# Block sums of four weight tiles made ahead in the memory-key stage, and two more seven-product pairs in the first feed-forward's first group

## The chip, the cores and the metric

The kernel runs on one core of a Trainium2 chip. A core has a matrix engine (TensorE, PE in the profile, whose weight loads are shown apart as PEld), a vector engine (VectorE, DVE), an activation engine (ScalarE, ACT), a general one (GpSimd, POOL) and a sync engine (SP), which here only issues transfers; 16 DMA engines carry those. The metric is the device time of one execution in microseconds. Before the change the median of three runs is 2403.33 us (2403.15 to 2403.53).

## The reference

The reference is one layer of a streaming encoder block on 256 tokens of width 2048, in float32:

```python
x = x + 0.5 * swiglu(rms_norm(x, ffn1_norm[l]), ffn1_w_up[l], ffn1_w_down[l])
h = rms_norm(x, mix_norm[l])
proj = h @ w_in[l]
...
x = x + cross_attention(rms_norm(x, xattn_norm[l]), rms_norm(mem, mem_norm[l]), ...)
x = x + 0.5 * swiglu(rms_norm(x, ffn2_norm[l]), ffn2_w_up[l], ffn2_w_down[l])

def swiglu(h, w_up, w_down):
    gate, up = jnp.split(h @ w_up, 2, axis=-1)
    return (jax.nn.silu(gate) * up) @ w_down
```

Two parts matter here. The memory's keys are `rms_norm(mem) @ wkv[:, :2048]` for 256 memory tokens, and the first feed-forward multiplies 256 tokens by `w_up` of 2048 x 11264.

## The kernel before, in words

**Numbers.** TensorE multiplies a rounded type (fp32r). Each float32 operand is split into a high part, which ACT makes by rounding (`split`, L153), and a low part, which VectorE makes as the rest (L154). A product is then three matmuls: high by high, high by low and low by high. Weights come as tiles of 128 x 2048 (1024 KB), which SP loads into a buffer named `raw`; the high part goes to `h`, the low to `l`. Each of the three has three buffers; within the first feed-forward there is a fourth, `raw1`.

**The stream of weights.** All tiles of the kernel stand in one list, `plan`, in the order in which they are used: tiles 0 to 15 for the memory's values, 16 to 31 for the memory's keys (wk0 to wk15 below), and from 32 on the first feed-forward. `weights` hands them out and keeps two prepared ahead; `prepare` issues a tile's load, its split, and what else its kind needs. `rest[i]` hangs side work on tile i: in the keys these are the loads and operands of x for the first feed-forward (xf, xg, xs, xd). The order in which each engine takes its instructions, and the buffer that each tile gets, are fixed when the program is built; at run time each engine takes its instructions in that order and waits by semaphores.

**The memory's keys.** Each tile is one `product`: 16 matmuls of 512 columns with the high part (L370) and 16 of 256 columns with the low part (L373). The result is summed (ACT L412, VectorE L414), split (L438, L439) and after every second tile stored by POOL's queue (L988).

**The first feed-forward.** The up projection runs in 11 groups of 512 gate and 512 up columns. A group has eight tiles, called pairs, since each holds two blocks of 128 rows of the weights by two blocks of 512 columns. `FIRST` gives for each group the order of its pairs and the kind of each. A mixed pair ("m") is multiplied in the plain way, 8 products or 24 matmuls, from one split of its tile; its operands include a difference of two blocks of x ("less", xd), which is made for the pairs in `BOTH`. A fast pair ("f") needs 7 products, 21 matmuls, in the manner of Strassen's scheme, but sums of its four weight blocks: VectorE makes them in three instructions (`td`: L337 with 1024 columns, L339 and L341 with 512), ACT and VectorE split the upper 1536 columns of the tile (`h`, `l`) and the 2048 columns of the sums in two halves (`th`, `tl`). `three` issues the matmuls, highs at L709 and lows at L711. All products of a group add into eight banks of the accumulator memory; when a group is done, ACT and VectorE take them out (`ev`, L791 to L804), and the next group's banks come free by that.

**Sums made ahead.** In the second feed-forward some fast pairs are of a third kind, "ready" (`sums_ready`): their sums were made earlier, in the middle of the kernel, and are kept in device memory in a tile t. `make_ahead` does it: POOL's queue loads the tile (L224), VectorE makes four subtractions of 512 columns in place (L229), POOL's queue stores the result (L230). There it works in a pool of its own, `prep`, of two buffers. `beside` calls its steps between the tiles, one pair per four tiles, each finished three tiles after its start. A ready pair loads two raw tiles, the upper 1536 columns of its weights (768 KB) and t (1024 KB), and VectorE only makes the low parts.

Of the kernel before, what the change touches and what calls it, by code (L numbers as in the profile page):

```python
# [8 lines left out]
F32 = mybir.dt.float32  # L9
# [4 lines left out]
P = 128  # L14
# [5 lines left out]
NG = DFF // 512  # L20
# [22 lines left out]


PIECES = "f1 a3 f0 a4 f2 a5 a6 f7"
FIRST = ["m0 f1 m2 f3 f5 m4 f7 m6"] + ["f1 f3 M0 f4 f2 M6 f5 f7"] * 2 + ["f1 f3 M0 a4 f2 a5 a6 f7"] + [PIECES] * (NG - 4)
KINDS = {"m": "mixed", "M": "mixed", "f": "fast", "a": "fast"}


# [7 lines left out]
def first(g):  # L57
    return [(KINDS[e[0]], g, int(e[1])) for e in FIRST[g].split()]

# [22 lines left out]
def adds(name, e):  # L82

    return e[0] == "fast" and (name == "ffn1" or e[1] > 3) and f"a{e[2]}" in FIRST[e[1]]


def sums_ready(name, e):

    made = {0: (), 1: (6,), 2: (5, 7), 3: (5, 7)}.get(e[1], range(8))
    return name == "ffn2" and e[0] == "fast" and e[2] not in made  # L90

# [2 lines left out]
def block_kernel(ctx: ExitStack, tc: tile.TileContext, xT, xin, memT, vec, gfin, bgate, lruw, wu1, wd1, win, wv,  # L94
# [15 lines left out]
    scoped = {}  # L110
# [49 lines left out]
    plan, ahead, made_ahead = [], [], []  # L160
    orders = {"ffn1": ffn_order(), "ffn2": ffn_order(every=True)}

    def plan_ffn(name, wu, wd):
        for e in orders[name]:
            src = wd[e[4], e[3]] if e[0] == "down" else wu[e[1], e[2]]
            kind = "fast" if e[0] == "fast" else "plain"
            if name == "ffn1" and e[0] == "mixed" and f"M{e[2]}" in FIRST[e[1]]:
                kind = "added"
            if e[0] == "down" and e[4] < NG - 1 and e[4] % 2 == 0 and e[3] % 2 and (e[4] or name == "ffn1"):
                kind = "added"  # L170
            if kind == "fast" and name == "ffn2" and e[1] < 4:
                kind = "fast early"
            if adds(name, e):
                kind += " added"
            if sums_ready(name, e):
                kind = "ready"
                t = kept.tile([P, 2048], F32, name=f"t{e[1]}_{e[2]}")
                made_ahead.append((src, t))
                src = src, t
            plan.append(((name,) + e, src, kind))  # L180
# [15 lines left out]
    first_ffn = len(plan)  # L196
# [23 lines left out]

    def make_ahead(src, to):

        t = scoped["prep"].tile([P, 2048], F32, name="prep", tag="prep")
        nc.gpsimd.dma_start(t, src)  # L224
        yield
        b = [t[:, i * 512:(i + 1) * 512] for i in range(4)]
        with tc.issue_after(done["low"]):
            for o, x, y in ((1, 0, 1), (0, 0, 2), (2, 2, 1), (3, 3, 2)):
                dve.tensor_tensor(out=b[o], in0=b[x], in1=b[y], op=ALU.subtract)  # L229
        nc.gpsimd.dma_start(to, t)  # L230
        yield

    under_way = []

    def beside(i):

        if under_way and (i >= under_way[0][0] or "prep" not in scoped):
            next(under_way.pop(0)[1])
        if made_ahead and "prep" in scoped and i >= turn[0] and i < first_second - 4 and (
                not first_q - 12 <= i < first_q + 5):  # L240
            turn[0] = i + 4
            steps = make_ahead(*made_ahead.pop(0))
            next(steps)
            under_way.append((i + 3, steps))
# [5 lines left out]
    def weights(*key, most=2):  # L250
        while plan and len(ahead) < most:
            i = next(planned)
            k, src, kind = plan.pop(0)
            if i == 0:
                in_turn.enter_context(tc.manual_schedule(engines={sp.engine, act.engine, dve.engine}))
            if i == 0:
                begun.append(raw_tile())
                act.dma_start(begun[0][:, :512], in_blocks(src, 512)[:P])
            if i < len(head):
                head[i]()  # L260
            if plan and plan[0][2] == "added":
                begun.append(begin_added(plan[0][1]))
            ahead.append((k, prepare(src, kind, i if i < 4 else None)))
            if i in rest:
                rest[i]()
            beside(i)
            if i == 7:
                in_turn.close()
        k, w = ahead.pop(0)
        assert k == key, (k, key)  # L270
        return w
# [7 lines left out]
    def raw_tile():  # L279

        if "raw2" in scoped and next(loads) % 5 > 2:
            return scoped["raw2"].tile([P, 2048], F32, name="raw2", tag="raw2")
        if "raw1" in scoped and next(loads) % 4 == 3:
            return scoped["raw1"].tile([P, 2048], F32, name="raw1", tag="raw1")
        return rawp.tile([P, 2048], F32, name="raw", tag="raw")
# [285 lines left out]
        for z in range(2):  # L571
            act.activation(g[:, z * T:][:, :T], a[:, z * T:(z + 1) * T], ACT.Copy, scale=gain(k + z))

    BOTH = [0, 2, 4, 6]

    def operand_pairs(src, gain, q, xg, out, every=False):


        for a in src:
# [6 lines left out]
            if every and q == 3:  # L586
                if not i:
                    xd.append(slot(F32R, "xd"))
                less = [xd[-1][:, a:a + 256] for a in (512 * i, 512 * i + 256)]
            if not every and 2 * q + i in BOTH:  # L590
                n = 512 * (BOTH.index(2 * q + i) % 2)
                if not n:
# [133 lines left out]
    def ffn(name, pairs, sq, then, begin=(), sums=()):  # L726
# [38 lines left out]
        for at, e in enumerate(order):  # L765
# [3 lines left out]
            if kind != "down":  # L769
# [3 lines left out]
                for i, (a, b, n) in enumerate(PRODUCTS["ready" if sums_ready(name, e) else kind]):  # L773
                    u = uses[g, n]
                    if u[0] == (p, i):
                        accs[n] = bank()
                    own, less = pairs[p]
                    products.append((accs[n], part(own, a, P) if a >= 0 else part(less, -1 - a, P), part(w[b // 4] if fast else w, b % 4, 512),
                                     u[0] == (p, i), u[-1] == (p, i)))
# [826 lines left out]
```

## Time and profile before

| | before |
|---|---|
| median of 3 runs | 2403.33 us |
| the profiled execution: its time / its span | 2403.28 / 2401.5 us |
| TensorE busy | 2391.5 us, 12044 matmuls |
| VectorE busy | 2081.6 us |
| ACT busy | 1568.6 us |
| memory's keys begin on TensorE at | about 94 us |
| first feed-forward begins on TensorE at | 182.66 us |
| second group of the first feed-forward at | 224.02 us |

Times in the rows are microseconds from the start of the span. A row of the timeline is: start, duration, engine, line, operation, output and inputs by the program's names, type and shape; in brackets at its end stand the idle time just before it and what ended it. Matmuls overlap, so a duration of 0.39 us does not mean that the next one starts 0.39 us later. A row of transfers gives what is loaded, the queue, the size, and the time from issue to landing.

### The profile page before, as it was taken

The numbers are of one execution on the slowest core, as the hardware profiler recorded it, in microseconds if no ns is written. First come the engines' busy times: TensorE is split into PE (matmuls) and PEld (weight loads), VectorE is DVE, ScalarE is ACT, GpSimd is POOL, SyncE is SP. The second block draws the span as 40 slices with busy tenths as digits, with TensorE's granted clock in tenths as the row PEclk, the third lists the DMA queues.
The fourth block names the chain that finished last, engine by engine and source line by source line (L and its number), as shares of the span: only waits on it lengthen the run. The fifth ranks groups of instructions, "written<-read, shape, count | busy, mean of one in ns | idle before, by whom it ended". The sixth has DMA issues, their size and how long they took to land.

```text
span 2401.5 us, 31008 instructions
## 1 busy us (share of the span) xinstructions
PE 2391.5 (100%) x12044; PEld 1990.1 (83%) x12044; DVE 2081.6 (87%) x2368; ACT 1568.6 (65%) x1609; POOL 120.2 (5%) x174
## 2 busy tenths in 40 slices
PE   9999999999999999999999999999999999999998
PEld 8888888888888888888888888888888888888887
DVE  7769999999999878778778888876799999999995
ACT  7756777777777665445457556655676677777774
POOL 0000000000000000000000000010000000000000
PEclk9999999999999999999999999999999999999999
DMA  8876888898999755676776868885687899999993
GB/s 310 310 248 224 270 268 266 273 277 273 276 277 276 264 190 208 250 270 254 276 307 250 315 241 268 301 297 216 212 332 292 317 277 276 273 278 273 265 278 133
DMA packets 98740, 640.04 MB, mean 267 GB/s; under 512 B 10976, under 2 KB 11488, under 8 KB 32928
## 3 DMA queue, kind: packets, MB, share of 16 engines
q1 hardware_dynamic: 74160, 493.61, 54.8%
q0 software_dynamic: 24288, 144.19, 24.6%
q8 instruction: 94, 1.54, 0.2%
q14 instruction: 54, 0.44, 0.0%
q10 hardware_dynamic: 144, 0.26, 0.0%
HBM read 601.18 MB, written 36.83 MB: 266 GB/s over the span
## 4 chain that ended last, share of the span: by engine, by line
PE 97%; DVE 2%; DMA 1%; issue 0%; ACT 0%; ACTq 0%; DVEq 0%
PE acc L709 39%; PE acc L711 20%; PE acc L370 11%; PE acc L396 6%; PE acc L397 6%; PE acc L402 6%; PE acc L373 6%; PE acc L749 1%; PE acc L554 1%; DVE l L154 0%; DVE tl L154 0%; DMA raw<-wq 0%; PE acc L1368 0%; PE acc L1112 0%; PE acc L1393 0%
## 5 line engine op out<-in xcount | busy, mean ns | idle before, releaser
L153 ACT ACTIVATE h<-raw 128x2048 fp32r<-128x2048 f32 (+3 forms) x423 | 684.8, 1633 | 400.0 <-PE acc L397 115.5
L154 DVE TENSOR_TENSOR l<-raw,h 128x2048 fp32r<-128x2048 f32 (+2 forms) x365 | 749.3, 2054 | 197.2 <-ACT h L153 193.9
L709 PE MATMUL acc<-h,xh 128*128 128x512 f32 x1221 | 474.2, 391 | 0.7 <-ACT h L153 0.6
L709 PE MATMUL acc<-h,xl 128*128 128x512 f32 x1221 | 473.8, 390 | 0.0
L153 ACT ACTIVATE h<-td 128x1024 fp32r<-128x1024 f32 x290 | 304.6, 1056 | 177.8 <-PE acc L709 65.2
L154 DVE TENSOR_TENSOR tl<-td,h 128x1024 fp32r<-128x1024 f32 x290 | 352.3, 1220 | 13.1 <-ACT h L153 11.3
L709 PE MATMUL acc<-h,hidop 128*128 128x512 f32 x1408 | 351.7, 391 | 0.0
L709 PEld LDWEIGHTS acc<-h,hidop 128*128 128x128 f32 x1408 | 262.7, 188 | 54.0
L709 PEld LDWEIGHTS acc<-h,xh 128*128 128x128 f32 x1221 | 229.2, 188 | 53.4 <-ACT h L153 4.7
L709 PEld LDWEIGHTS acc<-h,xl 128*128 128x128 f32 x1221 | 229.3, 188 | 46.5
L370 PE MATMUL acc<-ops,h 128*128 128x512 f32 x896 | 218.0, 393 | 0.0
L396 PE MATMUL acc<-h,ops 128*128 128x512 f32 x512 | 201.2, 393 | 0.0
L397 PE MATMUL acc<-h,ops 128*128 128x512 f32 x512 | 199.4, 390 | 0.0
L711 PE MATMUL acc<-tl,xh 128*128 128x512 f32 x660 | 193.6, 395 | 0.1
L370 PEld LDWEIGHTS acc<-ops,h 128*128 128x128 f32 x896 | 164.0, 188 | 32.4
L711 PE MATMUL acc<-l,hidop 128*128 128x512 f32 x704 | 190.6, 389 | 0.0
L337 DVE TENSOR_TENSOR td<-raw 128x1024 f32<-128x1024 f32 x149 | 181.6, 1218 | 3.5 <-DMA raw<-wout 2.3
L711 PE MATMUL acc<-l,xh 128*128 128x512 f32 x561 | 157.0, 390 | 0.0
L711 PEld LDWEIGHTS acc<-l,hidop 128*128 128x128 f32 x704 | 132.1, 188 | 27.6
L711 PEld LDWEIGHTS acc<-tl,xh 128*128 128x128 f32 x660 | 120.2, 188 | 34.4 <-DVE tl L154 11.0
L402 PE MATMUL acc<-l,ops 128*128 128x512 f32 x512 | 126.6, 389 | 0.0
L711 PEld LDWEIGHTS acc<-l,xh 128*128 128x128 f32 x561 | 105.3, 188 | 22.4
(276 smaller groups left out, 3094.8 us busy)
## 6 DMA issues: line engine op xcount, KB each, us to landing
raw<-wu SPq DMA_DIRECT2D x151, 1024.0 KB, 7.1
raw<-wd SPq DMA_DIRECT2D x88, 1024.0 KB, 7.4
l<-wu POOLq DMA_DIRECT2D x59, 768.0 KB, 8.5
raw<-win SPq DMA_DIRECT2D x40, 1024.0 KB, 4.8
raw<-wg SPq DMA_DIRECT2D x32, 1024.0 KB, 5.8
prep<-wu POOLq DMA_DIRECT2D x25, 1024.0 KB, 6.6
t<-prep POOLq DMA_DIRECT2D x25, 1024.0 KB, 4.7
raw<-t SPq DMA_DIRECT2D x25, 1024.0 KB, 6.2
```

The costliest lines, as they stand in the source:

```text
L153: done["high"] = act.activation(h, raw, ACT.Copy).ins
L154: done["low"] = dve.tensor_tensor(out=l, in0=raw, in1=h.bitcast(F32), op=ALU.subtract).ins
L337: dve.tensor_tensor(out=two[0], in0=raw[:, None, :512].broadcast_to([P, 2, 512]), in1=two[1], op=ALU.subtract)
L370: pe.matmul(acc, h[:, k * P:(k + 1) * P], xs[k], start=k == 0, stop=False)
L373: done["product"] = pe.matmul(acc[:, :T], l[:, k * P:(k + 1) * P], xs[k][:, :T], start=False, stop=k == KT - 1).ins
L396: pe.matmul(accs[t], x[:, t * P:][:, :P], h[j], start=first and j == 0, stop=False)
L397: pe.matmul(accs[t], x[:, T + t * P:][:, :P], h[j], start=False, stop=False)
L402: done["product"] = pe.matmul(accs[t], x[:, t * P:][:, :P], l[j], start=False, stop=last and j == 3).ins
L554: pe.transpose(acc[:, z * T + t * P:][:, :P], tile[:, t * 512 + (2 * y + z) * P:][:, :P], ident)
L709: pe.matmul(acc, a, b, start=start, stop=False)
L711: done["product"] = pe.matmul(acc, ah, bl, start=False, stop=stop).ins
L749: pe.transpose(acc[:, z * T + t * P:][:, :P], hid[t][:, (2 * y + z) * P:][:, :P], ident)
```

## The change

Four things are changed, and one follows from them.

1. In the first group of the first feed-forward the pairs 4 and 6, mixed before, become fast (`FIRST`).
2. The fast pairs 1, 3, 5 and 7 of that group become ready: their sums are made ahead. `beside` starts one of the four with each of the tiles wk1, wk5, wk9 and wk13, and finishes it two tiles later.
3. In this stage there is no `prep` pool, so `make_ahead` takes a tile from `raw_tile`, that is, one of the three raw buffers.
4. The operand "less" is no longer made for pair 4 (`BOTH`).

The line numbers from L240 on are nine higher in the changed kernel (L337 is L346, L709 is L718, L802 is L811); those of `split` are two higher (L153 is L155), `make_ahead` five (L229 is L234).

```diff
-FIRST = ["m0 f1 m2 f3 f5 m4 f7 m6"] + ["f1 f3 M0 f4 f2 M6 f5 f7"] * 2 + ...
+FIRST = ["m0 f1 m2 f3 f5 f4 f7 f6"] + ["f1 f3 M0 f4 f2 M6 f5 f7"] * 2 + ...
...
 def sums_ready(name, e):
 
+    if name == "ffn1":
+        return e[0] == "fast" and e[1] == 0 and e[2] in (1, 3, 5, 7)
     made = {0: (), 1: (6,), 2: (5, 7), 3: (5, 7)}.get(e[1], range(8))
     return name == "ffn2" and e[0] == "fast" and e[2] not in made
...
     def make_ahead(src, to):
 
-        t = scoped["prep"].tile([P, 2048], F32, name="prep", tag="prep")
+        if "prep" in scoped:
+            t = scoped["prep"].tile([P, 2048], F32, name="prep", tag="prep")
+        else:
+            t = raw_tile()
         nc.gpsimd.dma_start(t, src)
...
     def beside(i):
 
-        if under_way and (i >= under_way[0][0] or "prep" not in scoped):
+        if under_way and (i >= under_way[0][0] or "prep" not in scoped and i > first_ffn):
             next(under_way.pop(0)[1])
+        if i in range(first_ffn - 15, first_ffn, 4):
+            steps = make_ahead(*made_ahead.pop(0))
+            next(steps)
+            under_way.append((i + 2, steps))
...
-    BOTH = [0, 2, 4, 6]
+    BOTH = [0, 2, 6]
```

Three places of the engines' orders show how the instructions move. The first is POOL, which issues the transfers of its queue; before, in the stages of the memory's values (v, the last two of them) and keys (k):

```order
L971 DMA v6_137<-vs_964 128x1024
L971 DMA v7_138<-vs_970 128x1024
L988 DMA k0_123<-ops_960 128x1024
L988 DMA k1_124<-ops_1073 128x1024
L988 DMA k2_125<-ops_1179 128x1024
L988 DMA k3_126<-ops_1296 128x1024
L988 DMA k4_127<-ops_1390 128x1024
```

and now:

```order
L980 DMA v7_142<-vs_976 128x1024
L229 DMA raw_1152<-wu1 128x2048
L997 DMA k0_127<-ops_966 128x1024
L997 DMA k1_128<-ops_1084 128x1024
L229 DMA raw_1366<-wu1 128x2048
L997 DMA k2_129<-ops_1191 128x1024
L235 DMA t0_3_96<-raw_1152 128x2048
L997 DMA k3_130<-ops_1309 128x1024
L997 DMA k4_131<-ops_1405 128x1024
L229 DMA raw_1596<-wu1 128x2048
L235 DMA t0_5_97<-raw_1366 128x2048
```

Between the stores of the keys stand now the loads of the tiles made ahead (wu1 is the weight of the first feed-forward) and the stores of their sums (t0_3 is pair 3's of group 0).

The second is SP at the last key tiles, with the semaphores that each load waits for; DMAHW stands for completions of SP's own queue, DMASW for those of POOL's. Before, from wk11 to wk15 and m0:

```order
L310 DMA raw_1452<-wk 128x2048 [waits DMAHW2_49,DVE_49]
L310 DMA raw_1516<-wk 128x2048 [waits DMAHW3_49,DVE_49]
L876 DMA xf_1305<-xT 128x1024 [waits DMAHW1_49]
L310 DMA raw_1569<-wk 128x2048 [waits DMAHW4_49,DVE_49]
L310 DMA raw_1615<-wk 128x2048 [waits DMAHW5_49,DVE_49]
L310 DMA raw_1661<-wk 128x2048 [waits DMAHW6_49,DVE_49]
L310 DMA raw_1707<-wu1 128x2048 [waits DMAHW0_49,DVE_49]
```

and now, from wk11 to wk15, m0, f1 with its sums, and m2:

```order
L319 DMA raw_1468<-wk 128x2048 [waits DMASW3_49,DMASW0_49,DVE_49]
L319 DMA raw_1537<-wk 128x2048 [waits DMAHW4_49,DVE_49]
L319 DMA raw_1590<-wk 128x2048 [waits DMAHW6_49,DVE_49]
L319 DMA raw_1638<-wk 128x2048 [waits DMAHW0_49,DVE_49,Activation_49]
L319 DMA raw_1684<-wk 128x2048 [waits DMAHW2_49,DMASW6_49,DMASW4_49]
L319 DMA raw_1735<-wu1 128x2048 [waits DMAHW1_49,DVE_49]
L335 DMA raw_1794<-wu1 128x1536 [waits DMAHW2_49,DVE_49]
L337 DMA raw_1796<-t0_1_95 128x2048 [waits DMAHW5_49,DMAHW3_49,DVE_49]
L319 DMA raw_1836<-wu1 128x2048 [waits DMAHW4_49,DVE_49]
```

The loads of wk11 and of wk15 wait now for transfers of POOL's queue, and between m0 and m2 stand two loads in place of one.

The third is VectorE in the first group. Before, from f1's sums to f3's:

```order
L337 TENSOR_TENSOR td_1768<-raw_1766 128x1024
L339 TENSOR_TENSOR td_1768<-raw_1766,td_1768 128x512
L341 TENSOR_TENSOR td_1768<-raw_1766,td_1768 128x512
L154 TENSOR_TENSOR tl_1777<-td_1768,h_1776 128x1024
L337 TENSOR_TENSOR td_1842<-raw_1840 128x1024
L154 TENSOR_TENSOR l_1812<-raw_1810,h_1811 128x2048
L154 TENSOR_TENSOR tl_1777<-td_1768,h_1776 128x1024
L339 TENSOR_TENSOR td_1842<-raw_1840,td_1842 128x512
```

and now, from m2's low part to f4's sums:

```order
L156 TENSOR_TENSOR l_1838<-raw_1836,h_1837 128x2048
L156 TENSOR_TENSOR l_1871<-raw1_1866,h_1870 128x1536
L156 TENSOR_TENSOR tl_1875<-raw_1868,h_1874 128x1024 x2
L156 TENSOR_TENSOR l_1909<-raw_1904,h_1908 128x1536
L156 TENSOR_TENSOR tl_1913<-raw_1906,h_1912 128x1024 x2
L346 TENSOR_TENSOR td_1941<-raw1_1939 128x1024
L348 TENSOR_TENSOR td_1941<-raw1_1939,td_1941 128x512
L156 TENSOR_TENSOR l_1946<-raw1_1939,h_1945 128x1536
L350 TENSOR_TENSOR td_1941<-raw1_1939,td_1941 128x512
```

Sums (td) stood with every second pair before; now the first of them in the group are f4's, behind the low parts of m2, f3 and f5.

More of the change, by code (lines that the diff above doesn't have):

```diff
@@ L45 @@
 PIECES = "f1 a3 f0 a4 f2 a5 a6 f7"
-FIRST = ["m0 f1 m2 f3 f5 m4 f7 m6"] + ["f1 f3 M0 f4 f2 M6 f5 f7"] * 2 + ["f1 f3 M0 a4 f2 a5 a6 f7"] + [PIECES] * (NG - 4)
+FIRST = ["m0 f1 m2 f3 f5 f4 f7 f6"] + ["f1 f3 M0 f4 f2 M6 f5 f7"] * 2 + ["f1 f3 M0 a4 f2 a5 a6 f7"] + [PIECES] * (NG - 4)
 KINDS = {"m": "mixed", "M": "mixed", "f": "fast", "a": "fast"}
```

## The prediction

> **What bounds the kernel now.** I read the busy shares and the chain of waits on the page first, then the table of busy time by stretch for the two places that the change touches: the memory's keys (about 94 to 183 us) and the first feed-forward's first group (from 183 us).
>
> ```profile
> PE 2391.5 (100%) x12044; PEld 1990.1 (83%) x12044; DVE 2081.6 (87%) x2368; ACT 1568.6 (65%) x1609; POOL 120.2 (5%) x174
> PE 97%; DVE 2%; DMA 1%; issue 0%; ACT 0%; ACTq 0%; DVEq 0%
> ...
> 100.00:200.00 100.00, 100.00 (x554) 87.11 (x553) 72.47 (x99) 56.84 (x75) 5.33 (x10) 1.00 0.75 255
> 182.66:230.00 47.34, 47.34 (x209) 38.60 (x208) 44.57 (x45) 31.27 (x28) 1.42 (x2) 1.00 0.71 232
> ```
>
> TensorE is busy for 2391.5 of 2401.5 us, so a removed matmul is a gain and an added wait of TensorE is a loss, nearly one for one. The last two rows (columns: span, then busy time of PE, PEld, DVE, ACT and POOL, granted clock, DMA share, GB/s) say where slack is: in the keys VectorE works 72% of the time and the transfers take 75% of the engines' time; in the first group VectorE works 44.57 of 47.34 us. The change takes subtractions out of the second stretch, puts two "fast" pairs into it, and loads the first.
>
> **The gain: six matmuls.** A pair by eight products is 24 matmuls, by seven 21.
>
> ```profile
> 218.58 0.39 PE L709 MATMUL acc<-h,xh 128*128 128x512 f32 x1
> 224.02 0.39 PE L709 MATMUL acc<-h,xh 128*128 128x512 f32 x1
> ```
>
> These are the first matmuls of m6 and of the next group's first pair: 5.44 us for 24, so 0.2267 us each. Two pairs turned from m to f give 6 x 0.2267 = 1.36 us. That TensorE has nothing else to win is seen from the one wait in this stretch, quoted below: 0.60 us.
>
> **VectorE's bill in the first group.** The distance from one start to the next is what an instruction costs on this engine (the first five rows; the last three are ACT's, for the high parts):
>
> ```profile
> 204.73 2.28 DVE L154 TENSOR_TENSOR l<-raw,h 128x2048 fp32r<-128x2048 f32 x1
> 206.93 1.22 DVE L154 TENSOR_TENSOR tl<-td,h 128x1024 fp32r<-128x1024 f32 x1
> 208.06 0.69 DVE L339 TENSOR_TENSOR td<-raw,td 128x512 f32<-128x512 f32 x1
> 208.66 1.75 DVE L154 TENSOR_TENSOR l<-raw,h 128x1536 fp32r<-128x1536 f32 x1
> 210.33 0.69 DVE L341 TENSOR_TENSOR td<-raw,td 128x512 f32<-128x512 f32 x1
> 136.46 1.91 ACT L153 ACTIVATE h<-raw 128x2048 fp32r<-128x2048 f32 x1 [0.57 <-PE acc L370]
> 231.14 1.06 ACT L153 ACTIVATE h<-td 128x1024 fp32r<-128x1024 f32 x1 [0.18 <-DVE td L341]
> 232.85 1.50 ACT L153 ACTIVATE h<-raw 128x1536 fp32r<-128x1536 f32 x1 [0.17 <-ACT hidop L753]
> ```
>
> So 2048 columns cost 2.20 us, 1536 cost 1.67, 1024 cost 1.13 and 512 cost 0.60. A mixed pair is 2.20. A fast pair is 1.13 + 0.60 + 0.60 for its sums, 1.67 and 2 x 1.13 for its low parts: 6.26. A ready pair needs no sums: 1.67 + 2.26 = 3.93. Before, the group (m0 f1 m2 f3 f5 m4 f7 m6) is 4 x 2.20 + 4 x 6.26 = 33.8; now (m0, four ready, m2, f4, f6) 2 x 2.20 + 4 x 3.93 + 2 x 6.26 = 32.6. Over the whole group VectorE is hardly relieved: what the four ready pairs save (4 x 2.33 = 9.3) f4 and f6 take back (2 x 4.06 = 8.1). And the work is later: the ready pairs stand at the front, the pairs with sums to make at the end. ACT gets 1.50 + 2 x 1.06 in place of 1.91 for each new fast pair, 3.4 us in a stretch where it works 31.27 of 47.34; that and the operand that BOTH no longer makes, in the keys, are within slack and count nothing.
>
> **The keys: sixteen subtractions and 8.4 MB.** Each of the four tiles made ahead costs four subtractions, a 1 MB load and a 1 MB store on POOL's queue.
>
> ```profile
> L229 DVE TENSOR_TENSOR prep<-prep 128x512 f32<-128x512 f32 x100 | 68.9, 689 | 1.9
> 132.81 2.29 DVE L154 TENSOR_TENSOR l<-raw,h 128x2048 fp32r<-128x2048 f32 x1 [1.41 <-ACT h L153]
> 171.52 3.82 PE L370 MATMUL acc<-ms,h 128*128 128x512 f32 x16
> 177.09 3.82 PE L370 MATMUL acc<-ms,h 128*128 128x512 f32 x16
> 182.66 0.40 PE L709 MATMUL acc<-h,xh 128*128 128x512 f32 x1
> ```
>
> The first row is the same step as it runs later in the kernel: 16 x 0.60 to 0.69 = 10 to 11 us. VectorE idles 27.5 of 100 us here, so they fit. On POOL's queue the stores of the memory's keys stand behind t's stores, which wait for the subtractions; nobody reads those keys before the cross attention, so that costs nothing but the traffic. A key tile costs TensorE 5.57 us (171.52 to 177.09), and its split waits for ACT, which waits for TensorE to release a high buffer (the second row here, and the 0.57 us ahead of ACT's row at 136.46): there is time to spare, as long as the raw tile has landed.
>
> That is what I doubt. The stage has only three raw buffers; the tiles made ahead take them too, and each is held from its load until its store has landed. In the order of SP's issues the load of wk11 now waits for t3's store and that of wk15 for t5's (the completions of POOL's queue in its waits), and by the buffers that the build gives, wk9 and wk10 follow each other in one buffer, and so do wk11, wk13 and wk14. SP issues in order: the loads behind wait as well. The chain, by the rows of before: wk9's split ends at 132.81 + 2.29 = 135.1, t3's last subtractions and a sum behind it at about 137.1. Then t3's store (S); wk11's load (D) and split (h 1.91 on ACT, l 2.29: 4.2); wk13's load (D) and split (4.2, and up to q = 2 because t5's four subtractions stand ahead of it on VectorE); wk14's load (D) and its high part (1.9). The high part of wk14 is ready at 137.1 + S + 3D + 10.3 + q. TensorE wants it at 171.5.
>
> ```profile
> raw<-wk SPq DMA_DIRECT2D x16, 1024.0 KB, 5.3
> xf<-xT SPq DMA_DIRECT2D x1, 512.0 KB, 7.1
> v<-vs POOLq DMA_DIRECT2D x1, 512.0 KB, 7.7
> raw<-wk SPq DMA_DIRECT2D x1, 1024.0 KB, 7.1
> raw<-wk SPq DMA_DIRECT2D x1, 1024.0 KB, 8.0
> t<-prep POOLq DMA_DIRECT2D x25, 1024.0 KB, 4.7
> 110.00:120.00 10.00, 10.00 (x57) 8.71 (x57) 7.45 (x9) 7.41 (x15) 0.53 (x1) 1.00 1.05 376
> 130.00:140.00 10.00, 10.00 (x61) 8.90 (x60) 6.06 (x8) 5.35 (x6) 0.53 (x1) 1.00 0.83 295
> ```
>
> DMA rows give the time from issue to landing: a key tile takes 5.3 in the middle case and 7.1 or 8.0 in windows where POOL's queue moves something too; t's store takes 4.7 where the queues are emptier. Bounds: S = 4.7, D = 5.3, q = 0 gives 168.0, no stall. When t3's store is issued wk10 (1024 KB), xf, two key stores (512 KB each) and t3 itself are in flight by the order, 3.7 million bytes; at the 376 GB/s of the fullest window that is 9.8 us, so S = 9.8, D = 7.1, q = 2 gives 180.5, a stall of 9.0. I take S = 8 (near v's 7.7 beside other transfers), D = 6 (between 5.3 and 7.1, since 130 to 140 us is at 83% before 2 MB per four tiles come on top) and q = 2: 137.1 + 8 + 18 + 10.3 + 2 = 175.4, a wait of **3.7 to 3.9 us, taken as 3.7**.
>
> [...]
>
> **The first group.** TensorE starts it at P (182.66 before).
>
> ```profile
> raw<-wu SPq DMA_DIRECT2D x1, 1024.0 KB, 7.6
> 189.57 2.29 DVE L154 TENSOR_TENSOR l<-raw,h 128x2048 fp32r<-128x2048 f32 x1
> 203.58 1.23 DVE L337 TENSOR_TENSOR td<-raw 128x1024 f32<-128x1024 f32 x1 [0.31 <-PE acc L711]
> 214.16 2.29 DVE L154 TENSOR_TENSOR l<-raw,h 128x2048 fp32r<-128x2048 f32 x1 [0.78 <-ACT h L153]
> 216.95 1.76 DVE L154 TENSOR_TENSOR l<-raw,h 128x1536 fp32r<-128x1536 f32 x1 [0.43 <-ACT h L153]
> 226.76 1.22 DVE L802 TENSOR_TENSOR ev<-acc,ev 128x1024 f32<-128x1024 f32 x1
> 228.10 0.62 PE L709 MATMUL acc<-h,xh 128*128 128x512 f32 x2
> 232.25 0.50 PE L709 MATMUL acc<-h,xh 128*128 128x512 f32 x1 [0.60 <-ACT h L153]
> ```
>
> Before, m2's low part started at P + 6.9 and from then on VectorE worked to L802, whose end (1.13 behind its start, 227.89) gives back the bank that the next group's first pair writes at 228.10: just in time. Now a ready pair takes two raw tiles (0.75 and 1 MB), and m2's raw buffer is that of f1's. With the numbers above t5's subtractions end near 160, its store at 168, wk15's load at 174 and its split at 178.2; f1's load lands 7.0 later (7.6 is the row beside other work, 5.3 the middle), its parts take 1.50 on ACT and 1.75, to 188.4, that is P + 2.0 with P = 182.66 + 3.7. m2's load lands at P + 9.0, and its low part starts at P + 10.9 (with 5.3 us loads and no stall P + 7, with 8 us P + 12).
>
> From there to the end of the same evacuation (L811 now) VectorE's row of instructions is m2 2.20, f3 3.93, f5 3.93, f4 6.26, f7 3.93, f6 6.26, the next pair 6.26, and 6.49 of the evacuation and the pair behind it (0.60 + 1.67 + 0.16 + 3 x 0.60 + 1.13 + 1.13): 39.3, with 1.5 of idle time, as the three waits in the rows come to (0.31 + 0.78 + 0.43; bounds 0 and 3). The bank is free at P + 10.9 + 39.3 + 1.5 = P + 51.7, before at P + 45.2, used at P + 45.4. TensorE, counted in the order, has then 8 matmuls fewer to go (1.8 us), and the 0.60 wait falls away: (51.8 - 45.4) - 1.8 - 0.6 = **+4.0**; with the bounds of idle time +2.5 to +5.5, with m2 at P + 7 (and 1.5 idle) about 0. The 1.36 is in this. On the way the waits show already in f6 and the next pair, whose sums come last. Behind the first groups nothing differs, so the shift stays to the end.
>
> **Sum.** 2403.28 (the profiled execution, against a median of 2403.33) + 3.7 + 4.0 = **2411 us**.
>
> **Rivals.** *Only the first group pays* (0.17): the keys' transfers land like the middle ones, TensorE does not wait for wk14, but f1 and m2, with six loads in a few us, are slow: 2403.3 + 4 = 2407. For it: 5.3 as the middle of sixteen. Against: what is added on the queues.
>
> *Nothing is slower* (0.17): the decisive point is the landing of a 1 MB load from 135 us on. At or under 5.3 us, with t3's store at 4.7, wk14 is ready before 171.5 and m2's low part starts at P + 7 or earlier; then the bank is free at P + 47.8 and the sum of the section above is 0, to 1.4 + 0.6 better if VectorE runs without idle time: 2401.3 to 2404, I say 2403. For it speaks that the step runs later in the kernel once per four tiles without a wait of TensorE (40.00 of 40 us busy), here with one load and two stores:
>
> ```profile
> 990.00:1030.00 40.00, 40.00 (x471) 35.21 (x469) 33.65 (x55) 19.05 (x21) 1.61 (x3) 1.00 0.66 241
> ```
>
> Against it: there it has a buffer of its own, and the transfers take 66% of the engines' time with its share in it.
>
> *The transfers are slow all the way* (0.16): 9.0 in the keys by the upper bound, and then m2 at P + 12.9 (wk15 180, f1 P + 3.0, 8.0 and 1.9), 6.0 in the group: 2418.
>
> ```profile
> core 0: 2401.5 us, clock 0.999
> ```
>
> [...]
>
> **How the numbers follow.** Forecast 0.50, the rivals as given. A measurement of this kernel can tell some 0.2%, 4.8 us: 2398.5 to 2408.1. Faster would need more than the six matmuls give: 0.02. Within: the case that costs nothing, and two thirds of the one at 2407, 0.26 with what of the forecast lands so low. Slower: 0.72. The range reaches from the light end of the second case to the slow one: 2404 to 2419; the forecast's own is 2408 to 2415.
>
> **What would show it.** In the profile after: a wait of TensorE of 2 to 6 us ahead of the first matmul of wk14 near 172 us, released by ACT's h; key loads of 6 us and more from 135 us on; m2's low part (L156) about 11 us behind TensorE's first matmul of the group; waits of TensorE in f6 and the next group's first pair, released by VectorE or ACT, which together come to about 6 us; and everything from 260 us on as before. It would be wrong if TensorE has no wait between 160 and 182 us, if the waits come at another tile (wk6 or wk11), or if VectorE has idle time between m2's low part and L811 of several us.

## The result, and the profile after

The changed kernel takes 2422.78 us (median of 6 runs, 2421.85 to 2424.28) against 2403.90 for the kernel before in the same series: a ratio of 1.0078, with a 95% interval of 1.0068 to 1.0088. It is slower, as forecast, but by 18.9 us where 7.7 were forecast; it lies above the range. The profiled execution took 2421.85 us, its span 2420.1, which is 18.6 more than the span before.

The page of the changed kernel, its busy shares and the shares of the chain of waits, then the busy time by stretch, with the same columns as before the change:

```profile
PE 2398.2 (99%) x12038; PEld 1990.9 (82%) x12038; DVE 2089.0 (86%) x2379; ACT 1569.0 (65%) x1612; POOL 124.5 (5%) x182
PE 88%; DVE 5%; DMA 4%; issue 1%; ACT 1%; SPq 0%; POOL 0%; ACTq 0%; DVEq 0%; POOLq 0%
...
100.00:200.00 100.00, 92.53 (x501) 80.37 (x500) 66.17 (x97) 47.48 (x68) 9.09 (x17) 0.95 0.79 281
195.40:242.74 47.34, 44.97 (x191) 34.60 (x189) 38.87 (x34) 30.24 (x28) 1.43 (x2) 1.00 0.93 329
```

The six matmuls are gone (12038 against 12044), yet TensorE is busy 6.7 us longer, and in the keys it has lost clock (0.95 over 100 to 200 us). In the first group VectorE is busy for only 38.87 of 47.34 us: it starts late. The loss has two parts, which the start of the group separates. The timeline of TensorE:

```profile
161.19 6.41 PE L379 MATMUL acc<-ms,h 128*128 128x512 f32 x16 [5.56 <-ACT h L155]
182.56 5.53 PE L379 MATMUL acc<-ms,h 128*128 128x512 f32 x16 [1.92 <-ACT h L155]
195.40 0.40 PE L718 MATMUL acc<-h,xh 128*128 128x512 f32 x1
248.34 0.47 PE L718 MATMUL acc<-h,xh 128*128 128x512 f32 x1 [1.21 <-DVE ev L811]
```

TensorE waits 5.56 us for wk11 and 1.92 for wk14, and after each wait the 16 matmuls take 6.41 and 5.53 us where they take 3.82 undisturbed. The group begins at 195.40 in place of 182.66, **12.7 us** later. Nearly all of it is lost in the keys: from the first matmul of wk0 to that of the group TensorE takes 101.31 us in place of 89.04, which is 12.3 more; the other 0.5 is there before the keys begin (94.09 against 93.62). In the nine profiles here in which TensorE does not wait in the keys the stage takes 89.04 us each time, so the start of the keys is what differs between executions; in the runs that lose time there it moves the group's start by -0.1 to +0.5 us. The rest, 18.6 - 12.7 = **5.9 us**, is lost in the first and second group.

Where the keys' loss comes from stands in the chain of waits (start, duration, what):

```profile
113.33 10.86 DMA raw<-wk
...
125.39 8.28 DMA raw<-wk
...
138.40 0.55 POOL raw L229
...
144.74 8.78 DMA t<-raw
153.57 5.64 DMA raw<-wk
...
173.01 2.21 DVE l L156
175.27 5.30 DMA raw<-wk
180.60 1.92 ACT h L155
```

From 144.74 on this is the chain of the prediction, link by link: t3's store, wk11's load, its parts, and from wk13's split (173.01) to wk14's load and its high part, which TensorE takes at 182.56. What is ahead of it was not in the prediction: loads of 8 to 11 us, and the subtractions of t3 late behind them. POOL's timeline, SP's wait for a store of t between 98 and 114 us and its issue behind it, and VectorE's timeline show why:

```profile
106.00 0.53 POOL L235 DMA_DIRECT2D t<-raw  x1 [17.76 <-DVE raw L234]
110.22 0.54 POOL L229 DMA_DIRECT2D raw<-wu  x1 [0.28 <-issue]
...
SPq L319 <- DMA t<-raw: 9.2, 1, 9.2
...
112.77 0.33 SPq L319 DMA_DIRECT2D raw<-wk  x1
...
135.70 2.29 DVE L156 TENSOR_TENSOR l<-raw,h 128x2048 fp32r<-128x2048 f32 x1 [4.17 <-ACT h L155]
138.84 1.41 DVE L234 TENSOR_TENSOR raw<-raw 128x512 f32<-128x512 f32 x2
140.17 2.29 DVE L156 TENSOR_TENSOR l<-raw,h 128x2048 fp32r<-128x2048 f32 x1
...
143.65 0.68 DVE L234 TENSOR_TENSOR raw<-raw 128x512 f32<-128x512 f32 x1
```

t1's store is issued at 106.0 and the load of wk6, which has its buffer, waits for it: it goes out at 112.77 (101.73 before the change), and wk7's right behind it at 113.33 (107.32 before). With t3's load (110.22) beside them they take 8.3 and 10.86 us (4.9 and 5.2 before). The chain of waits goes through wk7's 10.86 us; what holds wk8's load back is wk6, whose buffer it has: wk6's load lands at 121.1, its low part ends at 125.36, and wk8's load goes out at 125.39 (112.87 before). t3 is loaded from 110.2 on, but its subtractions stand in VectorE's order behind wk8's low part (135.70) and, the last two, behind wk9's (140.17), and both are late. So t3 keeps its raw buffer until its store lands at 153.5, and from 138.4 on POOL's next load (t5) has another: for 15 us one of three is left to the keys.

### The profile page after: what moved, and what is told of

Read it like the earlier page. It is cut to its first block, busy times and chain, and to the rows that moved or that the text cites. A ratio compares the mean times of both kernels' runs of the same rounds, so it can differ in the third digit from the quotient of the medians.

```text
span 2420.1 us, 31040 instructions
## 1 busy us (share of the span) xinstructions
PE 2398.2 (99%) x12038; PEld 1990.9 (82%) x12038; DVE 2089.0 (86%) x2379; ACT 1569.0 (65%) x1612; POOL 124.5 (5%) x182
## 4 chain that ended last, share of the span: by engine, by line
PE 88%; DVE 5%; DMA 4%; issue 1%; ACT 1%; SPq 0%; POOL 0%; ACTq 0%; DVEq 0%; POOLq 0%
PE acc L718 36%; PE acc L720 18%; PE acc L379 9%; PE acc L405 5%; PE acc L411 5%; PE acc L406 5%; PE acc L382 5%; DVE l L156 2%; DMA raw<-wk 1%; DMA raw<-wout 1%; ACT h L155 1%; DVE tl L156 1%; PE acc L758 1%; PE acc L563 0%; DVE td L346 0%
## 5 line engine op out<-in xcount | busy, mean ns | idle before, releaser
L155 ACT ACTIVATE h<-raw 128x2048 fp32r<-128x2048 f32 (+3 forms) x431 | 691.4, 1620 | 423.9 <-PE acc L406 117.5
L718 PE MATMUL acc<-h,xh 128*128 128x512 f32 x1223 | 475.8, 392 | 3.5 <-ACT h L155 1.4
L718 PE MATMUL acc<-h,xl 128*128 128x512 f32 x1223 | 474.4, 390 | 0.0
L155 ACT ACTIVATE h<-td 128x1024 fp32r<-128x1024 f32 x286 | 300.2, 1055 | 173.8 <-PE acc L718 63.0
L718 PE MATMUL acc<-h,hidop 128*128 128x512 f32 x1408 | 351.7, 391 | 0.0
L718 PEld LDWEIGHTS acc<-h,hidop 128*128 128x128 f32 x1408 | 262.7, 188 | 54.1
L718 PEld LDWEIGHTS acc<-h,xh 128*128 128x128 f32 x1223 | 229.6, 188 | 59.3 <-ACT h L155 6.4
L718 PEld LDWEIGHTS acc<-h,xl 128*128 128x128 f32 x1223 | 229.7, 188 | 46.5
L346 DVE TENSOR_TENSOR td<-raw 128x1024 f32<-128x1024 f32 x147 | 179.2, 1219 | 3.5 <-DMA raw<-wout 2.6
```

The source lines that it names most:

```text
L155: done["high"] = act.activation(h, raw, ACT.Copy).ins
L346: dve.tensor_tensor(out=two[0], in0=raw[:, None, :512].broadcast_to([P, 2, 512]), in1=two[1], op=ALU.subtract)
L718: pe.matmul(acc, a, b, start=start, stop=False)
```

## The experiments

Each was timed against the kernel before in the same series; ratios have their 95% interval. P is the start of the first group on TensorE. What the keys lose is given as the shift of P against 182.66, and so holds the start of the keys too (-0.1 to +0.5 us).

**One raw buffer held, no transfers** (hold_one).

```diff
 def beside(i):
...
+    if i == first_ffn - 15:
+        holding.append(raw_tile())
+        dve.memset(holding[0][:, :512], 0.0)
+    if i == first_ffn - 1:
+        with tc.issue_after(done["low"]):
+            dve.tensor_tensor(out=holding[0][:, :512], in0=holding[0][:, :512],
+                              in1=holding[0][:, :512], op=ALU.subtract)
```

> The kernel before, in which one raw buffer is taken from wk1 to wk15 and nothing is done with it but two small writes of VectorE; its computation is unchanged. Theory A (the keys' loss comes from two tiles made ahead that hold two of three raw buffers at once, while loads take 8 to 11 us): one buffer held is free, since the high part of a tile can be made 8.8 us ahead of its use and a buffer needs 5.3 + 4.2 us of 11.1 per round; 2403 to 2404.5 us, no wait of TensorE in the keys. Theory B (any raw buffer taken from the keys starves TensorE): waits in the keys, 5 us and more, 2409 to 2416. Theory C (the transfers alone): no change.

2403.37 us, ratio 0.9999 (0.9990 to 1.0009). The table of stretches:

```profile
100.00:180.00 80.00, 80.00 (x458) 70.56 (x457) 56.55 (x83) 46.57 (x66) 4.80 (x9) 1.00 0.76 267
```

TensorE is busy for all of the 80 us. Two raw buffers are enough for the keys, with loads of 5.7 us in the middle case: theory B falls.

**The transfers alone** (traffic).

```diff
             if m % 2:
                 nc.gpsimd.dma_start(kept_k[m // 2], ks.cur)
+                if m < 15:
+                    for z in range(2):
+                        nc.gpsimd.dma_start(kept.tile([P, 1024], F32, name=f"u{m}_{z}"), kept_k[m // 2])
```

> The kernel before, in which POOL's queue copies each stored pair of the memory's keys twice more within device memory (14 copies of 512 KB, read and written, 7 MB beside the change's 8.4), without a buffer of the core; the copies are not used. Theory C (the added transfers alone slow the key tiles until TensorE waits): loads of key tiles of 7 us and more and waits, 2406 to 2415 us. Theories A and B: loads get longer, some to 7 or 8 us, and nothing waits: 2403 to 2405.

2403.64 us, ratio 0.9999 (0.9989 to 1.0008). The transfers from 100 to 180 us and the stretch:

```profile
raw<-wk SPq DMA_DIRECT2D x10, 1024.0 KB, 7.5
...
100.00:180.00 80.00, 80.00 (x459) 70.57 (x458) 56.37 (x81) 47.22 (x67) 9.32 (x18) 1.00 0.89 320
```

Key loads take 7.5 us at 320 GB/s, and TensorE does not wait once: with three buffers loads of this length are hidden. Theory C falls as the only cause.

**Holds and subtractions without the transfers** (hold_subs).

```diff
 def beside(i):
...
+    if holding and i == holding[0][0]:
+        b = [holding.pop(0)[1][:, j * 512:(j + 1) * 512] for j in range(1)] * 4
+        with tc.issue_after(done["low"]):
+            for o, x, y in ((1, 0, 1), (0, 0, 2), (2, 2, 1), (3, 3, 2)):
+                dve.tensor_tensor(out=b[o], in0=b[x], in1=b[y], op=ALU.subtract)
+    if i in range(first_ffn - 15, first_ffn, 4):
+        t = raw_tile()
+        dve.memset(t[:, :512], 0.0)
+        holding.append((i + 2, t))
```

> The kernel before, with raw buffers taken at wk1, wk5, wk9 and wk13, filled by a write of VectorE and released by four subtractions two key tiles later: the change's holds and subtractions without its six transfers. The results of these are not used. Theory A (a buffer is held until the store has landed, and the loads that wait for it are slow beside the store): without the transfers the holds end with the subtractions and the loads land in 5 to 6 us; no wait of TensorE, or under 1 us: 2403 to 2405. If the subtractions or the holds alone are enough: waits in the keys, 2408 to 2415.

2403.94 us, ratio 0.9999 (0.9990 to 1.0008), no wait of TensorE in the keys. The subtractions cost nothing there, and neither do holds that end with them. (Without the transfers the build gives the buffers out in another order, so this is not the change less one thing alone.)

**The tiles made ahead in a low buffer** (in_low).

```diff
         else:
-            t = raw_tile()
+            t = lp.tile([P, 2048], F32, name="made", tag="l")
```

> The change, with the tiles made ahead in a buffer of the low parts (l) and not in a raw one. Theory A: the key tiles keep three raw buffers, so no load of a key waits for POOL's store; with two low buffers left a low part can still be made a tile ahead; the keys lose 0 to 2 us, the first group some 5: 2407 to 2411 us. Theory C: 2415 to 2423, with key loads of 7 us and more and waits at wk11 and wk14.

2407.48 us, ratio 1.0017 (1.0008 to 1.0027). The stretch of the keys, the start of the group, and what it waits for in the second group:

```profile
100.00:180.00 80.00, 80.00 (x460) 70.60 (x459) 62.43 (x91) 45.02 (x65) 7.81 (x15) 1.00 0.87 325
...
183.58 0.40 PE L718 MATMUL acc<-h,xh 128*128 128x512 f32 x1
...
235.08 0.47 PE L718 MATMUL acc<-h,xh 128*128 128x512 f32 x1 [1.22 <-DVE ev L811]
```

The same sums, transfers and pairs, and the keys lose nothing: the loss there is that of the raw buffers, held until the transfers have landed, since holds that ended with the subtractions cost nothing (hold_subs). How much the slower key loads beside the transfers add to it is not shown: no run holds the buffers as long without the transfers. What is left, 3.8 us (4.9 in the profiled execution), is the first group's loss alone, and its bank comes free at P + 51.5.

**The same, finished a tile earlier** (in_low_one): `under_way.append((i + 1, steps))` in place of `i + 2`.

> The same, finished one key tile after the start. Theory A: like in_low or a little better, 2406 to 2410 us, no wait of TensorE in the keys. What is left then is the first group's loss alone, 3 to 6 us.

2408.09 us, ratio 1.0021 (1.0012 to 1.0031): not to be told from the one above.

**The change, finished a tile earlier**, in the raw buffers (finish_one), by the same edit:

> The change, with each tile made ahead finished one key tile after its start and not two, so that it holds its raw buffer shorter. Theory A (two of these tiles hold two buffers at once): most of the overlap goes, the keys lose 0 to 3 us in place of 12.7, the first group 5 to 6 as before: 2408 to 2413 us. Theory C (the transfers): the same transfers, so the same loss: 2420 to 2424.

2415.78 us, ratio 1.0051 (1.0036 to 1.0066). TensorE's waits in the keys:

```profile
155.31 3.92 PE L379 MATMUL acc<-ms,h 128*128 128x512 f32 x16 [0.45 <-ACT h L155]
175.32 3.92 PE L379 MATMUL acc<-ms,h 128*128 128x512 f32 x16 [2.19 <-ACT h L155]
186.56 0.40 PE L718 MATMUL acc<-h,xh 128*128 128x512 f32 x1
```

With the same transfers the keys lose 3.9 us in place of 12.7, so the transfers alone are not the cause; that it is the length of the holds is only partly shown. t3's and t5's buffers are held for 28 and 30 us (43 and 39 in the change), but t1's for 44 (32 in the change): its subtractions come at 113.6, where in the change they came at 102.5. Two of three buffers are still held at once, by t1 and t3, for 15 us, but early, from 108.5 to 124.0. The keys lose a little more than the 0 to 3 us that I expected, and the whole is 2.8 us above the upper bound, since the group loses 6.8 in this profile (2412.2 - 2401.5 - 3.9), more than in the change.

**Three tiles made ahead, f1's sums made in the group** (three_ahead).

```diff
-        return e[0] == "fast" and e[1] == 0 and e[2] in (1, 3, 5, 7)
+        return e[0] == "fast" and e[1] == 0 and e[2] in (3, 5, 7)
...
-        if i in range(first_ffn - 15, first_ffn, 4):
+        if i in range(first_ffn - 11, first_ffn, 4):
```

> The change with the sums of pairs 3, 5 and 7 alone made ahead, at the same key tiles; f1 makes its own in the group. If the keys lose because the first of the tiles (t1) delays wk6 and with it everything to t3's subtractions (144.3 us in the change against 137.1 in the prediction's chain), this start is back where the prediction had it: wk11 in time, wk14 ready at 175 us and not 182.6, TensorE begins the first group at 184 to 188 us (195.4 in the change, 182.7 before). If one tile less changes nothing but the transfers, since t3 and t5 still hold two buffers at once: 192 to 196. In the group VectorE has 34.9 us of pairs in place of 32.6, so some 2 more are lost there: in all 2410 to 2415, against 2418 to 2424.

2416.12 us, ratio 1.0052 (1.0035 to 1.0069).

```profile
132.84 2.14 DVE L234 TENSOR_TENSOR raw<-raw 128x512 f32<-128x512 f32 x3
135.25 0.68 DVE L234 TENSOR_TENSOR raw<-raw 128x512 f32<-128x512 f32 x1
...
174.27 5.51 PE L379 MATMUL acc<-ms,h 128*128 128x512 f32 x16 [2.27 <-ACT h L155]
187.10 0.40 PE L718 MATMUL acc<-h,xh 128*128 128x512 f32 x1
```

Without t1, t3's subtractions end at 135.9, wk11 is in time, wk14 is ready at 174.3 (the prediction had 175.4) and the group begins at 187.1 (186.4). The links of the prediction's chain fit once its start does. That the group's start fits so well has some luck in it: wk14 is ready 1.1 us sooner than the prediction has it, and its 16 matmuls lose 1.7 us of clock that the prediction leaves out. The group loses 12.4 - 4.4 = 8.0, so the sum is 1 us above the expectation.

**Matmuls that nobody uses, ahead of wk11 and wk14** (filler).

```diff
         for m in range(KT):
...
+            wk_m = weights("k", m)
+            if m in (11, 14):
+                spare, many = bank("spare"), 24 if m == 11 else 8
+                for j in range(many):
+                    pe.matmul(spare, ms.tiles[j % KT][:, :P], ms.tiles[j % KT][:, :512], ...)
...
```

> The change with matmuls that nobody uses ahead of wk11 (24 of them, 5.4 us) and of wk14 (8, 1.8 us), where TensorE waits 5.56 and 1.92 us. [...]

2424.07 us, ratio 1.0086 (1.0071 to 1.0101).

```profile
156.14 5.63 PE L997 MATMUL spare<-ms 128*128 128x512 f32 x24
161.60 3.79 PE L379 MATMUL acc<-ms,h 128*128 128x512 f32 x16
...
183.53 5.28 PE L379 MATMUL acc<-ms,h 128*128 128x512 f32 x16 [3.25 <-ACT h L155]
```

Kept busy, TensorE does wk11's matmuls in 3.79 us and not in 6.41; the granted clock is 1.00 from 156 to 168 us. The 2418 to 2420 us that I expected of this did not come: what was won at wk11 is waited for at wk14 (3.25 us), whose high part comes at 183.5 as it came at 182.6. So the wait at wk11 and the clock lost there are not on the path at all; the group's start is set by wk14's data and what the clock loses there.

**The eight ahead of wk14 alone** (filler_14).

> The change with eight matmuls that nobody uses (1.8 us) ahead of wk14 alone, in the wait of 1.92 us there. wk14's data set when it starts, so the wait at wk11 and its lost clock come back as that wait at wk14. If idling costs the clock, wk14's 16 matmuls take 3.8 in place of 5.5 us and the group begins at 193.7 in place of 195.4: 2420.5 to 2422 us. If the clock falls there anyway (for the idling at wk11, or because the wait at wk14 is longer than the eight matmuls): 2422 to 2424, 195 to 196.

2421.60 us, ratio 1.0074 (1.0059 to 1.0089).

```profile
159.10 5.52 PE L379 MATMUL acc<-ms,h 128*128 128x512 f32 x16 [4.10 <-ACT h L155]
...
180.27 3.94 PE L379 MATMUL acc<-ms,h 128*128 128x512 f32 x16 [0.77 <-ACT h L155]
```

With a wait of 0.77 us left, wk14's matmuls take 3.94 us and not 5.53. P is 191.53, 3.9 us earlier than in the change; 1.6 of these are the clock, the other 2.3 wk14's data, which came earlier in this execution. The first groups take most of it back: they lose 2418.5 - 2401.5 - 8.9 = 8.1 us where they lost 5.9, so the span is 1.6 us shorter. In the times alone 1.2 us less is not to be told from the change.

**The old order of the group, sums made ahead** (old_first; `FIRST` and `BOTH` as before the change).

> The change without its first part: the four sums are made ahead, pairs 4 and 6 of the first group stay mixed. Theory A: the keys lose as in the change, 12.7 us with what the clock loses, and the first group loses nothing, since VectorE has 24.5 us of pairs to prepare in place of 32.6; only the 0.6 us wait goes: 2414 to 2417 us. If the first group's loss came from the late loads of f1 and m2 and not from VectorE's row of work: 2418 to 2421.

2414.23 us, ratio 1.0043 (1.0028 to 1.0058). The keys lose 10.4 us (P is 193.04), the group 0.8, in one wait of 1.6 for ACT. Take the two pairs back to eight products, and the group's loss is gone, though m2's low part starts at P + 8.9, no earlier than in in_low (P + 8.5), which loses 3.8: it was VectorE's row of work.

**The two pairs, no sums made ahead** (no_ahead; `sums_ready` and `beside` as before).

> The change without the sums made ahead: pairs 4 and 6 are fast, all six fast pairs make their sums in the group. The keys run as before, TensorE begins the group at 182.7 us. VectorE has 2 x 2.20 + 6 x 6.26 = 42.0 us of pairs in place of 33.8, so it is 8 us late, against which stand 2.8 us of its idle time and matmuls for 1.4 us: waits of TensorE in the last pairs and the second group, 2407 to 2411 us. If ACT or the loads set the pace instead, waits are released by them and the time is under 2406.

2412.26 us, ratio 1.0036 (1.0023 to 1.0049), P at 182.79. TensorE's two longest waits:

```profile
227.47 0.79 PE L714 MATMUL acc<-l,xh 128*128 128x512 f32 x1 [1.54 <-DVE l L154]
...
230.18 0.80 PE L712 MATMUL acc<-h,xh 128*128 128x512 f32 x1 [1.06 <-ACT ev L794]
182.66:230.00 47.34, 43.44 (x182) 33.35 (x180) 45.59 (x44) 29.62 (x27) 1.42 (x2) 0.97 0.57 192
```

They stand where the group's last pairs and the next are, as expected; the time is 1 us above the upper bound. The granted clock falls to 0.97 in this stretch: the matmuls behind the two waits take 0.79 and 0.80 us, where one at 223.46 takes 0.39. 0.03 of 47.34 us is 1.4 us, so a part of the loss is the clock. Making sums ahead does help the group (8.2 us of loss here, 3.8 with them in a low buffer), but it does not pay for two pairs.

**All six pairs' sums ahead**, in low buffers, one every second tile (six_ahead).

```diff
-        return e[0] == "fast" and e[1] == 0 and e[2] in (1, 3, 5, 7)
+        return e[0] == "fast" and e[1] == 0 and e[2] in (1, 3, 4, 5, 6, 7)
...
-        if i in range(first_ffn - 15, first_ffn, 4):
+        if i in range(first_ffn - 15, first_ffn - 3, 2):
...
-            under_way.append((i + 2, steps))
+            under_way.append((i + 1, steps))
```

> The sums of all six fast pairs of the first group made ahead, in a buffer of the low parts, one every second key tile, each finished one tile after its start. If VectorE's row of work from m2's low part on is what the first group loses by, it has 2 x 2.20 + 6 x 3.93 = 28.0 us of pairs in place of 32.6: most of the 3.8 us of in_low come back, 2402 to 2405 us. If the late loads set it (two raw tiles for each ready pair, six in a row now): 2407 to 2412. The keys should lose nothing, with 12.6 MB on top.

2425.90 us, ratio 1.0091 (1.0076 to 1.0107). TensorE's and VectorE's waits (in total, times, longest):

```profile
PE acc L382 <- DVE l L156: 9.5, 8, 2.8
...
DVE l L156 <- DMA t<-made: 11.5, 5, 5.2
```

The expectation fails: the keys lose 15.2 us (P is 197.82), now because the low parts wait for a low buffer that t's store still reads. It is the same thing in another pool. So this run says nothing of the group.

**Sums of 3, 4, 5 and 6 ahead**, in low buffers (later_four; `e[2] in (3, 4, 5, 6)`).

> in_low with the sums of pairs 3, 4, 5 and 6 made ahead in place of 1, 3, 5 and 7: f1 makes its own sums, in VectorE's idle time at the end of the keys, as before, and takes one raw tile. VectorE has as much to do as in the change, but f1's part earlier and m2's load sooner: 2403 to 2406 us by VectorE's row of work. If the sums at the group's end (f7's and the next pair's) decide alone: as in_low, 2407 to 2409.

2411.50 us, ratio 1.0033 (1.0020 to 1.0045). VectorE's timeline at the start of the group, and TensorE's longest wait there:

```profile
183.92 0.69 DVE L234 TENSOR_TENSOR made<-made 128x512 f32<-128x512 f32 x1 [4.20 <-DMA made<-wu]
191.92 1.76 DVE L156 TENSOR_TENSOR l<-raw,h 128x1536 fp32r<-128x1536 f32 x1 [1.47 <-DMA t<-made]
...
197.32 0.79 PE L718 MATMUL acc<-h,xh 128*128 128x512 f32 x1 [4.58 <-ACT h L155]
```

This fails too. In the profiled execution, the slowest of the five (2408.32 to 2415.83), the keys lose nothing, but VectorE waits 4.2 us for the load of the last tile made ahead, which stands in its order ahead of m0's low part, then for that tile's store, and f1's own sums come 4.58 us late for TensorE. The last of the steps must be out of the way before the group's own work.

**One pair turned**, in low buffers (one_fast; `FIRST[0]` is "m0 f1 m2 f3 f5 f4 f7 m6").

> in_low with one mixed pair less turned: f4 is fast, pair 6 stays mixed. VectorE has 3 x 2.20 + 4 x 3.93 + 6.26 = 28.6 us in place of 32.6, TensorE 3 matmuls fewer than before: 2402 to 2404.5 us. If the late loads cost it: 2406 to 2408.

2403.42 us, ratio 0.9998 (0.9989 to 1.0007).

```profile
183.08:230.42 47.34, 47.34 (x210) 38.80 (x209) 41.90 (x39) 30.95 (x30) 1.43 (x2) 1.00 0.92 328
226.64 1.22 DVE L811 TENSOR_TENSOR ev<-acc,ev 128x1024 f32<-128x1024 f32 x1
```

TensorE has no wait in the group, and the bank is back at P + 44.7, earlier than before the change; m2's low part starts at P + 6.4 here, 2 us earlier than in in_low, which is part of it. Three matmuls fewer are 0.7 us, which this measurement does not show. It is the best of these kernels, and no better than the kernel before as far as the times tell.

## Why the prediction was right or wrong

**Right**: slower, and for the two reasons given, the raw buffers held in the keys and VectorE's row of work in the group. That the bank's return limits the second group, that a wait costs nearly its own length, and that hardly anything differs behind the first groups were as described. The six matmuls were saved and lost again.

**Wrong: the start of the chain in the keys.** "The chain, by the rows of before: wk9's split ends at 132.81 + 2.29 = 135.1, t3's last subtractions and a sum behind it at about 137.1." The two times were taken from a kernel in which no tile was made ahead. In the change t1's store holds up wk6 by 11.0 us (112.77 against 101.73), wk8 gets wk6's buffer, and the four loads from wk6 to wk9, which the sum does not have, take 8.3 to 10.9 us (4.9 to 7.1 before). wk9's low part ends at 142.5 and not at 135.1; t3's subtractions stand behind wk8's and wk9's: their end is 144.3, and the store goes out at 144.7, 7.6 us later than the chain has it. The same rule that I applied to t3 and wk11 was not applied to t1 and wk6, though SP waits for a store of t there too. Behind this the terms nearly fit: S was 8.8 (8 taken), the three loads 5.6, 4.9 and 5.3 (6 each), q 2.6 (2 taken), and wk14 was ready at 182.5 in place of 175.4. three_ahead, without t1, is at 174.3. The keys lose 12.3 - 3.7 = 8.6 us more than forecast. This step is 6.7 of them, counted from the start of the keys (182.5 - 175.4 = 7.1, less 0.5); the clock is 1.7, and 0.2 is the rounding from 3.9 to 3.7.

**Wrong: the clock was left out.** The forecast has no term for it; over the whole span before, the granted clock is 0.999. After the change the 16 matmuls at wk14 took 5.53 us in place of 3.82: 1.7 us on the path, with the clock at 0.50 from 183.60 to 187.01. The wait ahead of them was only 1.92 us; one of 2.19 us in finish_one cost 0.1 (last section). The 2.6 us at wk11 are off the path, as filler shows.

**Wrong: where the wait would show.** I named wk14 and gave "wk6 or wk11" as what would prove the chain wrong. wk11 had about 2 us to spare in my own numbers (137.1 + 8 + 6 + 1.9 = 153.0 against 154.8, where TensorE took it before), which the late start used up. The first wait is at wk11; but the one that counts is at wk14.

**The group: the mechanism holds, the size is short.** TensorE's wait for VectorE's evacuation (L811) is there. m2's low part and the end of L811, in the timeline of VectorE after the change:

```profile
206.73 4.01 DVE L156 TENSOR_TENSOR l<-raw,h 128x2048 fp32r<-128x2048 f32 x2 [1.47 <-ACT h L155]
246.98 1.22 DVE L811 TENSOR_TENSOR ev<-acc,ev 128x1024 f32<-128x1024 f32 x1
```

The first is at P + 11.3 (10.9 forecast), the end of the second (1.13 behind its start) at P + 52.7 (51.7), and the bank is written at P + 52.9. By the prediction's own formula that is (52.9 - 45.4) - 1.8 - 0.6 = 5.1, against 4.0 forecast; measured are 5.9, and the last 0.8 lie behind it (0.2 in a wait at the transposes, L758); their cause stays open. in_low, with no loss in the keys, lost 3.8, against the 4.0.

**The rivals.** That only the first group pays was the fate of in_low, not of the change. "The transfers are slow all the way", 2418, came nearest in its number, but not in its mechanism: key loads of 7.5 us cost nothing by themselves (traffic, ratio 0.9999).

## What to carry to other kernels

A step that borrows a buffer from a rotating pool costs that buffer from its load to the landing of its store (t3's from 110.2 to 153.5 us), with every place in the engines' orders at which it queues in between; before a chain is worked out from the times of the profile before, each earlier use of the same borrowing must be put into it, from the first on. Work that is moved ahead to relieve an engine helps only as much as that engine's row of instructions gets earlier at the place where it is waited for: here the ready pairs stood at the front of the group, where VectorE had time, and the pairs with sums to make at its end. And an earlier wait can be bought off without any gain when a later one is set by the same data (filler: wk14's high part at 183.5 us as at 182.6 in the change).

## What the runs showed of the hardware

The granted clock fell at some waits of TensorE and not at others, and the length of the wait does not decide it alone. After waits of 5.56 (the change), 4.10 (filler_14) and 3.96 us (old_first) the next 16 matmuls took 6.41, 5.52 and 6.76 us in place of 3.82; so it was after 1.92 us (5.53, in the change) and 2.27 us (5.51, in three_ahead), while waits of 2.19 (3.92, in finish_one) and 2.71 us (3.94, in old_first) cost 0.1.

In the changed kernel the clock is 0.50 from 159.71 to 166.53 and from 183.60 to 187.01. The busy time in these two stretches:

```profile
159.71:166.53 6.82, 5.34 (x13) 4.18 (x14) 5.36 (x12) 5.02 (x7) 0.53 (x1) 0.50 0.33 130
183.60:187.01 3.41, 3.41 (x10) 2.63 (x9) 1.39 (x2) 2.10 (x2) 0.00 (x0) 0.50 0.56 150
```

The first begins within the wait of 5.56 us, which ends at 161.19, the second 1.04 us behind the end of the wait of 1.92 us, at 182.56. TensorE works for 5.34 and 3.41 us of them; half of that is 2.7 and 1.7 us, and the 16 matmuls took 2.6 and 1.7 us more than 3.82. In finish_one the clock is 1.00 from 173 to 186 us, with the wait of 2.19 us in it. Why a wait of 1.92 us cost the clock and one of 2.71 us did not, these runs do not show.

A 1 MB load took 5.3 us in the middle case before and 7.5 with 7 MB of copies beside it (traffic), and up to 10.86 in the change for one of two loads that were issued 0.6 us apart beside a load of POOL's queue.
